# Value and output-gate projections with weight tiles of 512 rows by 512 columns instead of 1024 by 256

## The chip, the core and the metric

The kernel runs on one core of a Trainium2 chip. The metric is the time of one execution on the device in microseconds (us), from its first to its last instruction and what the launch adds around it. TensorE (PE) multiplies; VectorE (DVE) and ScalarE (ACT) work on its results; GpSimd (POOL) and SyncE (SP) mostly issue transfers.

## What is computed

The reference is one layer of a backbone over 256 context rows and 2048 latent rows of 1024 columns. The part that the change touches is the combined input projection:

```python
hl = modulate(rmsnorm(xl, g_norm1[layer]), ml[0], ml[1])
hc = modulate(rmsnorm(xc, g_norm1[layer]), mc[0], mc[1])
pl = split_proj(hl @ w_in[layer])       # 512-column groups: B, C, x_in, q, k, v, o, and 16 gates
pc = split_proj(hc @ w_in[layer])
hm_c, hm_l = mlstm_bidir((pc[3], pc[4], pc[5], pc[7]), (pl[3], pl[4], pl[5], pl[7]), gate_b[layer])
yl = mixer(pl, hm_l, conv_rows, conv_w[layer], conv_b[layer], g_head[layer], w_out[layer])
...
def mlstm_out(h, o, g_head, dtype):
    hn = h * lax.rsqrt(jnp.mean(h * h, axis=-1, keepdims=True) + EPS) * g_head[None, :, None, :]
    ...
    return jax.nn.sigmoid(o) * hn
```

`v` is the value projection (columns 2560 to 3071 of `w_in`), `o` the output gate (columns 3072 to 3583). After the mixer follow the output projection, a router and a mixture of 16 experts with 256 tokens each, and a last RMSNorm.

## The kernel before

Every float32 product is made of three products in the fp32r type: the weight and the activation are each split into a high part (rounded by ACT) and a low part (the remainder, by DVE), and high by high, high by low and low by high are summed in PSUM.

The first part goes over four blocks of 512 latent rows (loop at L548); block 0 also takes the 256 context rows. The normalised rows lie transposed in SBUF as eight tiles of 128 features by 512 rows, `his` and `los`. Weights come as tiles of 1024 rows by 256 columns, 1 MB each: `wtile` (L407) loads one over the SP queue into one of two `wraw` slots, `split_w` (L89) makes `whi` on ACT and `wlo` on DVE in one of three slots each. Two helpers multiply. `wstat` (L411) holds the weights still and moves 512 rows of `h`: 24 products of 512 columns for a result tile. `hstat` (L422) holds 128 rows of `h` still and moves the 256 columns of the weight tile: 24 products of 256 columns for a result tile of 128 rows by 256 columns. `hstat` is used for `v` (L564 to L574) and `o` (L646 to L655), each as two weight tiles (`j`) with four row tiles (`t`) for each, and in block 0 two more row tiles of the context for `v` (L568). A block has 14 weight tiles: K, V, Q, O with two each, then two rounds of three for the convolution. Result tiles lie in the PSUM pool `pmm`, four banks (L149), which the gates (L293) and the modulation rows (`pq`, L633 and L641) use too.

`v` is copied by DVE into `V1s` (L574), from which the scan's state is updated (`state_update`, L435) and which ACT's queue stores to `PK`. `o` goes through a Sigmoid on ACT into `so` (two slots of 256 columns), is multiplied on POOL by the head gain (L653) and stored from ACT's queue to `PG` (L655). Ahead of each `o` tile stands `mod_tile` (L631), which computes 256 columns of a modulation row on DVE from a 1 MB tile of `w_mod`, loaded into the same `wraw` slots.

The order on each engine is not the program's: the context at L1273 has `schedule_with_timeline_sim=True`, so a planner puts the instructions in order by a timeline of its own and gives out the slots. From some 745 us the scan's second half and the output projection (`stage_b`, L703, products of 512 columns at L730 to L732) follow, then the router, then the experts: `psx` at L1192 to L1194 with products of 256 columns, and `down` (L1106) with products of 512 columns over four PSUM tiles in turn, 128 rows of `h` held and split weights moved.

Of the kernel before, what the change touches and what calls it, by code (L numbers as in the profile page):

```python
# [8 lines left out]
F32 = mybir.dt.float32  # L9
# [4 lines left out]
AF = mybir.ActivationFunctionType  # L14
# [5 lines left out]
P = 128  # L20
D = 1024
KD = D // P
SEQ = 2048
NCTX = 256
NH = 4
# [13 lines left out]
def kernel(ctx, tc, x, c, cx, c_ctx, w_mod, b_mod, g_norm1, g_norm2, w_in, w_out, conv_w, conv_b,  # L39
                       gate_b, g_head, w_router, w_gate_e, w_up_e, w_down_e, g_final, out):  # L40
    nc = tc.nc
    V, S, G, T = nc.vector, nc.scalar, nc.gpsimd, nc.tensor
# [3 lines left out]
    w_in = w_in[0]  # L46
# [11 lines left out]
    PG = [dram.tile([P, PKW - SO], F32, name=f"PG{i}") for i in range(NCH)]  # L58
# [25 lines left out]
    def load_w(src, rows, cols):  # L84
        raw = wrawp.tile([P, rows, cols], F32, name="wraw", tag="wraw")
        nc.sync.dma_start(raw, src)
        return raw

    def split_w(raw, rows, cols, after=None, after_lo=None):  # L89
        hi = whip.tile([P, rows, cols], F32R, name="whi", tag="whi")  # L90
        if after is not None:
            S.activation(hi[:, 0, 0:1], after, AF.Copy)
        S.activation(hi, raw, AF.Copy)  # L93
        lo = whip.tile([P, rows, cols], F32R, name="wlo", tag="wlo")
        if after_lo is not None:
            tc.keep_in_program_order(G.tensor_copy(lo[:, 0, 0:1], after_lo))
        V.tensor_sub(lo, raw, hi.bitcast(F32))  # L97
        return hi, lo
# [33 lines left out]
    ghb = con.tile([P, 512], F32, name="ghb")  # L132
# [11 lines left out]
    def pool(st, name, bufs, **kw):  # L144
        return st.enter_context(tc.tile_pool(name=name, bufs=bufs, reuse_waits="tile", **kw))

    hp = pool(left, "hT", 12)
    wl = pool(left, "p1l", 2)
    pmm = pool(left, "p1mm", 4, space=PSUM)  # L149
# [97 lines left out]
    hc, stc = ([], []), [None, None]  # L247
    h, sth = ([], []), [None, None]
# [158 lines left out]
    def wtile(n0):  # L407
        raw = load_w(w_in[:, n0:n0 + 256].rearrange("(k p) n -> p k n", p=P), KD, 256)
        return split_w(raw, KD, 256)

    def wstat(w, i, h, ntok):  # L411
        hi, lo = w
        his, los = h
        ps = pmm.tile([P, 512], F32, name="ps", tag="mm")
        for k in range(KD):
            wh = hi[:, k, i * P:(i + 1) * P]
            T.matmul(ps[:, :ntok], wh, his[k], start=k == 0, stop=False)  # L417
            T.matmul(ps[:, :ntok], wh, los[k], start=False, stop=False)  # L418
            T.matmul(ps[:, :ntok], lo[:, k, i * P:(i + 1) * P], his[k], start=False, stop=k == KD - 1)  # L419
        return ps  # L420

    def hstat(w, h, t):  # L422
        hi, lo = w
        his, los = h
        ps = pmm.tile([P, 512], F32, name="ps", tag="mm")
        for k in range(KD):
            hh = his[k][:, t * P:(t + 1) * P]
            T.matmul(ps[:, :256], hh, hi[:, k, :], start=k == 0, stop=False)  # L428
            T.matmul(ps[:, :256], hh, lo[:, k, :], start=False, stop=False)  # L429
            T.matmul(ps[:, :256], los[k][:, t * P:(t + 1) * P], hi[:, k, :], start=False, stop=k == KD - 1)  # L430
        return ps

    Cst = {}

# [32 lines left out]
    V1c = [V1cc[:, 0], V1cc[:, 1]]  # L467
# [80 lines left out]
    for blk in range(4):  # L548
        KT = wk.tile([P, NH, 512], F32, name="KT", bufs=1)
        for j in range(2):  # L550
            w = wtile(2048 + j * 256)
            if blk == 0:
                for i in range(2):
                    ps = wstat(w, i, hc, NCTX)
                    S.activation(KTc[:, j * 2 + i, :], ps[:, :NCTX], AF.Copy)
            for i in range(2):
                ps = wstat(w, i, h, 512)
# [3 lines left out]
            T.transpose(pv[:, :24], vrow2, ident[:24, :24])  # L561
            V.tensor_copy(vcol[:, 72:96], pv[:, :24])
        V1s = [wk.tile([P, NH, P + 1], F32, name="V1", bufs=4) for _ in range(4)]
        for j in range(2):  # L564
            w = wtile(2560 + j * 256)
            if blk == 0:
                for t in range(2):
                    ps = hstat(w, hc, t)  # L568
                    V.tensor_copy(V1c[t][:, j * 2:j * 2 + 2, 0:P], ps[:, :256].rearrange("p (h v) -> p h v", h=2))
            for t in range(4):  # L570
                if j == 0:
                    V.memset(V1s[t][:, :, P:P + 1], 1.0)
                ps = hstat(w, h, t)
                V.tensor_copy(V1s[t][:, j * 2:j * 2 + 2, 0:P], ps[:, :256].rearrange("p (h v) -> p h v", h=2))  # L574
        if blk == 0:
            gc = gates(hc, 2, None)
        gl = gates(h, 4, blk)
# [4 lines left out]
        for j in range(2):  # L582
            w = wtile(1536 + j * 256)
            for i in range(2):
                ps = wstat(w, i, h, 512)
                qt = wl.tile([P, 512], F32, name="qt", tag="hf", bufs=2)
                S.activation(qt, ps, AF.Copy, scale=P ** -0.5)
                for t in range(4):
                    o_ = QO + (j * 2 + i) * P
# [41 lines left out]
        def mod_tile(q, row=row):  # L631
            def ev_b(acc, dst=(ml2b if row == 2 else ml5b), q=q):
                pq = pmm.tile([P, 512], F32, name="pq", tag="mm")  # L633
                bq = wl.tile([1, 256], F32, name="bq", bufs=2)
                nc.gpsimd.dma_start(bq, b_mod[0:1, row * D + q * 256:row * D + (q + 1) * 256])
                T.matmul(pq[:, :256], ones, acc, start=True, stop=False)
                T.matmul(pq[:, :256], ones[0:1, :], bq, start=False, stop=True)
                S.activation(dst[:, q * 256:(q + 1) * 256], pq[:, :256], AF.Copy)

            def ev_c(acc, dst=(B2 if row == 3 else A2), q=q, v0=(40 if row == 3 else 48)):  # L640
                pq = pmm.tile([P, 512], F32, name="pq", tag="mm")  # L641
                for i in range(2):
                    T.matmul(pq[:, i:i + 1], acc[:, i * P:(i + 1) * P], ones[:, 0:1], start=True, stop=True)
                V.tensor_tensor(dst[:, q * 2:q * 2 + 2], vcol[:, v0 + q * 2:v0 + q * 2 + 2], pq[:, 0:2], op=ALU.add)
            mod_row_bcast(psm, wl, row, q, ev_b if row in (2, 5) else ev_c)
        for j in range(2):  # L646
            mod_tile(j)
            w = wtile(3072 + j * 256)
            for t in range(4):
                so = wl.tile([P, 256], F32, name="so", bufs=2)  # L650
                ps = hstat(w, h, t)
                S.activation(so, ps[:, :256], AF.Sigmoid)
                G.tensor_mul(so, so, ghb[:, j * 256:(j + 1) * 256])  # L653
                o_ = j * 256
                nc.scalar.dma_start(PG[blk * 4 + t][:, o_:o_ + 256], so)  # L655
        for j in range(2):
            mod_tile(2 + j)
            cs = []
            w = wtile(512 + j * 256)
            for i in range(2):  # L660
                ps = wstat(w, i, h, 512)
# [3 lines left out]
            w = wtile(1024 + j * 256)  # L665
            ys = []
            for i in range(2):
                ct = j * 2 + i
                ps = wstat(w, i, h, 512)
# [11 lines left out]
            w = wtile(j * 256)  # L681
            for i in range(2):
                ct = j * 2 + i
                y = ys[i]
                ps = wstat(w, i, h, 512)
# [3 lines left out]
        h = hnext  # L689
# [140 lines left out]
    for n_, k2 in enumerate((2, 3, 0, 1)):  # L830
        raw = load_w(w_out[k2 * 2 * P:(k2 + 1) * 2 * P, :].rearrange("(k p) n -> p k n", p=P), 2, D)
        if n_ < 3:
            hi = whip.tile([P, 2, D], F32R, name="whi", tag="whi")
            lo = whip.tile([P, 2, D], F32R, name="wlo", tag="wlo")
        else:
            hi = wk.tile([P, 2, D], F32R, name="whi3", bufs=1)
            lo = wk.tile([P, 2, D], F32R, name="wlo3", bufs=1)
# [159 lines left out]
    with tc.tile_pool(name="xw", bufs=2, reuse_waits="tile") as xraw, tc.tile_pool(name="xh", bufs=2, reuse_waits="tile") as xhi, \  # L997
# [159 lines left out]
        for e in range(NE):  # L1157
# [4 lines left out]
            for pr in range(npair):  # L1162
                n = 2 if pr < npair - 1 else NFT - 2 * (npair - 1)
                f0 = pr * 2
                ws = []
                for src in (w_gate_e, w_up_e):
                    raw = load_w(src[0, e][:, f0 * P:(f0 + n) * P].rearrange("(k p) n -> p k n", p=P), KD, n * P)
# [18 lines left out]
                for i in range(n):  # L1186
                    ps = pmm.tile([P, 2, 2 * P], F32, name="psx", tag="mm")
                    for m_ in range(2):
                        hi, lo = ws[m_]
# [10 lines left out]
                    hh = wk.tile([P, 2 * P], F32R, name="hh", bufs=4)  # L1200
# [76 lines left out]
```

## Time and profile before

| what | us |
|---|---|
| median of 3 runs | 2697.55 (2696.11 to 2704.61) |
| the profiled execution | 2698.35 |
| span of its instructions | 2696.3 |
| PE busy | 2615.3 (97%) |
| PE weight loads busy, beside the products | 2365.0 (88%) |
| DVE busy | 1584.3 (59%) |
| ACT busy | 1155.3 (43%) |

Products overlap in the records: the busy time of one (280 ns for 256 columns, 390 ns for 512) is from its start to its modelled end, while the next one starts earlier. What a product costs in a full stretch is the distance from its start to the start of the next, and that is read from the timeline.

### The profile page before, as it was taken

The page shows a single profiled execution, that of the slowest core. Times are in us where ns is not written, and L with a number is a line of the kernel's source. Part 1 is how long each engine was busy: PE and PEld are TensorE (multiplying, and loading weights), DVE is VectorE, ACT ScalarE, POOL GpSimd, SP SyncE. Part 2 cuts the span into 40 slices and gives each one's busy share as a digit, 9 for nine tenths or more (in the row PEclk, how much of TensorE's full clock was granted, in tenths as well). Part 3 has the DMA queues.
Part 4 walks back from the last instruction along what each step waited for, and adds up shares of the span by engine and source line. Part 5 has one row for each costly group of instructions (what it writes and reads, how often), then busy time and mean ns, then how long its engine had stood idle before and what let it go on. Part 6 is the DMA issues. An engine that isn't in the chain of part 4 may idle for free.

```text
span 2696.3 us, 42922 instructions
## 1 busy us (share of the span) xinstructions
PE 2615.3 (97%) x17570; PEld 2365.0 (88%) x17570; DVE 1584.3 (59%) x2570; ACT 1155.3 (43%) x1723; POOL 301.0 (11%) x345
## 2 busy tenths in 40 slices
PE   8999999999999999689999999999999999999997
PEld 4988888888878888579999999999999999999987
DVE  5356454554575665566566556656655665665684
ACT  3243333422534444354444444444444444444553
POOL 1010000000111111210011011001101100110231
PEclk9999999999999999889999999999999999999999
DMA  8444554645656655165666666666666666666894
GB/s 271 135 147 148 170 165 147 196 129 156 204 183 206 208 183 172 64 219 188 205 217 208 200 209 219 189 208 214 209 202 208 219 191 206 214 210 202 276 318 166
DMA packets 382532, 524.57 MB, mean 195 GB/s; under 512 B 15072, under 2 KB 322736, under 8 KB 380288
## 3 DMA queue, kind: packets, MB, share of 16 engines
q1 hardware_dynamic: 327968, 437.96, 50.0%
q10 hardware_dynamic: 43792, 46.55, 5.1%
q0 software_dynamic: 10576, 37.32, 5.0%
q8 instruction: 138, 2.26, 0.3%
q14 instruction: 58, 0.48, 0.1%
HBM read 449.05 MB, written 72.61 MB: 193 GB/s over the span
## 4 chain that ended last, share of the span: by engine, by line
PE 63%; DMA 3%; DVE 2%; issue 2%; ACT 0%; POOL 0%; POOLq 0%; DVEq 0%; SPq 0%; ACTq 0%
PE psx L1192 12%; PE psx L1194 11%; PE psx L1193 11%; PE ac L1117 6%; PE ac L1119 6%; PE ac L1118 6%; PE po L730 2%; PE po L732 2%; PE po L731 2%; DMA pk<-PK 1%; PE ptx L1055 1%; PE pl L766 1%; PE pb L514 1%; PE pa L510 1%; DMA ACC<-yv,idx 1%
## 5 line engine op out<-in xcount | busy, mean ns | idle before, releaser
L1192 PE MATMUL psx<-xh,whi 128*128 128x256 f32 x2816 | 788.9, 281 | 1.6 <-ACT whi L93 1.5
L1193 PE MATMUL psx<-xl,whi 128*128 128x256 f32 x2816 | 786.7, 280 | 0.9 <-DVE xl L1064 0.9
L1194 PE MATMUL psx<-xh,wlo 128*128 128x256 f32 x2816 | 787.5, 280 | 0.0
L97 DVE TENSOR_TENSOR wlo<-wraw,whi 128x2048 fp32r<-128x2048 f32 x248 | 532.0, 2156 | 307.8 <-ACT whi L93 304.7
L93 ACT ACTIVATE whi<-wraw 128x2048 fp32r<-128x2048 f32 x248 | 446.7, 1804 | 373.3 <-PE psx L1193 112.1
L1194 PEld LDWEIGHTS psx<-xh,wlo 128*128 128x128 f32 x2816 | 535.3, 190 | 0.1
L1193 PEld LDWEIGHTS psx<-xl,whi 128*128 128x128 f32 x2816 | 530.5, 188 | 3.3 <-DVE xl L1064 1.4
L1192 PEld LDWEIGHTS psx<-xh,whi 128*128 128x128 f32 x2816 | 528.7, 188 | 4.1 <-ACT whi L93 1.7
L1117 PE MATMUL ac<-dhi,hh 128*128 128x512 f32 x704 | 276.2, 392 | 0.0
L1118 PE MATMUL ac<-dlo,hh 128*128 128x512 f32 x704 | 274.7, 390 | 0.0
L1119 PE MATMUL ac<-dhi,hl 128*128 128x512 f32 x704 | 273.3, 390 | 0.0
L1077 DVE TENSOR_TENSOR dlo<-draw,dhi 128x2048 fp32r<-128x2048 f32 x96 | 202.9, 2114 | 114.2 <-ACT dhi L1075 114.2
L418 PE MATMUL ps<-hlo,whi 128*128 128x512 f32 (+1 forms) x672 | 259.6, 387 | 0.0
L419 PE MATMUL ps<-hhi,wlo 128*128 128x512 f32 (+1 forms) x672 | 259.0, 386 | 0.0
L417 PE MATMUL ps<-hhi,whi 128*128 128x512 f32 (+1 forms) x672 | 258.6, 388 | 0.0
L1147 POOL DMA_INDIRECT ACC<-yv,idx x28 | 82.8, 2956 | 1124.1 <-DVE yv L1142 1012.6
L1075 ACT ACTIVATE dhi<-draw 128x2048 fp32r<-128x2048 f32 x96 | 170.2, 1772 | 69.7 <-PE ac L1119 67.6
L1201 ACT ACTIVATE hh<-sgt 128x256 fp32r<-128x256 f32 x176 | 73.2, 417 | 263.0 <-DVE sgt L1197 263.0
L1196 ACT ACTIVATE sgt<-psx 128x256 f32<-128x256 f32 x176 | 65.4, 372 | 228.0 <-PE psx L1194 227.9
L1119 PEld LDWEIGHTS ac<-dhi,hl 128*128 128x128 f32 x704 | 132.1, 188 | 27.8
L428 PE MATMUL ps<-whi,hhi 128*128 128x256 f32 x544 | 156.0, 287 | 0.0
L429 PE MATMUL ps<-wlo,hhi 128*128 128x256 f32 x544 | 154.9, 285 | 0.0
(411 smaller groups left out, 3901.8 us busy)
## 6 DMA issues: line engine op xcount, KB each, us to landing
wraw<-in_w_gate_e_dram SPq DMA_DIRECT2D x80, 1024.0 KB, 6.2
wraw<-in_w_up_e_dram SPq DMA_DIRECT2D x80, 1024.0 KB, 5.5
draw<-in_w_down_e_dram SPq DMA_DIRECT2D x80, 1024.0 KB, 6.1
wraw<-in_w_in_dram SPq DMA_DIRECT2D x56, 1024.0 KB, 5.5
pk<-PK SPq DMA_DIRECT2D x16, 1284.0 KB, 7.7
xt<-in_x_dram SPq DMA_DIRECT2D x32, 512.0 KB, 5.5
wraw<-in_w_mod_dram SPq DMA_DIRECT2D x16, 1024.0 KB, 6.8
wm<-in_w_mod_dram SPq DMA_DIRECT2D x8, 1024.0 KB, 12.0
```

The costliest lines, as they stand in the source:

```text
L93: S.activation(hi, raw, AF.Copy)
L97: V.tensor_sub(lo, raw, hi.bitcast(F32))
L417: T.matmul(ps[:, :ntok], wh, his[k], start=k == 0, stop=False)
L418: T.matmul(ps[:, :ntok], wh, los[k], start=False, stop=False)
L419: T.matmul(ps[:, :ntok], lo[:, k, i * P:(i + 1) * P], his[k], start=False, stop=k == KD - 1)
L1077: V.tensor_sub(lo, raw, hi.bitcast(F32))
L1117: T.matmul(ac, hhs, dh[:, i, sl], start=f == 0, stop=False)
L1118: T.matmul(ac, hhs, dl[:, i, sl], start=False, stop=False)
L1119: T.matmul(ac, hls, dh[:, i, sl], start=False, stop=f == NFT - 1)
L1192: T.matmul(ps[:, m_], wh, xh[:, k], start=k == 0, stop=False)
L1193: T.matmul(ps[:, m_], wh, xl[:, k], start=False, stop=False)
L1194: T.matmul(ps[:, m_], lo[:, k, i * P:(i + 1) * P], xh[:, k], start=False, stop=k == KD - 1)
```

## The change

For `v` and `o` the two weight tiles of 1024 rows by 256 columns become two of 512 rows by 512 columns. `hstat` now makes the result tiles of all row tiles at once: for the first half of the rows it adds to each of them in turn, then for the second half. Each product moves 512 columns and fills a whole PSUM bank. `so` becomes 512 columns wide and shares the two slots of `cs`, the convolution's tile. The first two modulation tiles of a block now both stand ahead of `o`.

```diff
-    def hstat(w, h, t):
-        hi, lo = w
+    def whalves(n0):
+        ws = []
+        for kh in range(2):
+            raw = load_w(w_in[kh * 512:(kh + 1) * 512, n0:n0 + 512].rearrange("(k p) n -> p k n", p=P), 4, 512)
+            ws.append(split_w(raw, 4, 512))
+        return ws
+
+    def hstat(ws, h, ts):
         his, los = h
-        ps = pmm.tile([P, 512], F32, name="ps", tag="mm")
-        for k in range(KD):
-            hh = his[k][:, t * P:(t + 1) * P]
-            T.matmul(ps[:, :256], hh, hi[:, k, :], start=k == 0, stop=False)
-            T.matmul(ps[:, :256], hh, lo[:, k, :], start=False, stop=False)
-            T.matmul(ps[:, :256], los[k][:, t * P:(t + 1) * P], hi[:, k, :], start=False, stop=k == KD - 1)
-        return ps
+        pss = [pmm.tile([P, 512], F32, name="ps", tag="mm") for _ in ts]
+        for kh, (hi, lo) in enumerate(ws):
+            for t, ps in zip(ts, pss):
+                for k4 in range(4):
+                    k = kh * 4 + k4
+                    hh = his[k][:, t * P:(t + 1) * P]
+                    T.matmul(ps, hh, hi[:, k4, :], start=k == 0, stop=False)
+                    T.matmul(ps, hh, lo[:, k4, :], start=False, stop=False)
+                    T.matmul(ps, los[k][:, t * P:(t + 1) * P], hi[:, k4, :], start=False, stop=k == KD - 1)
+        return pss
...
-        for j in range(2):
-            w = wtile(2560 + j * 256)
-            if blk == 0:
-                for t in range(2):
-                    ps = hstat(w, hc, t)
-                    V.tensor_copy(V1c[t][:, j * 2:j * 2 + 2, 0:P], ps[:, :256].rearrange("p (h v) -> p h v", h=2))
-            for t in range(4):
-                if j == 0:
-                    V.memset(V1s[t][:, :, P:P + 1], 1.0)
-                ps = hstat(w, h, t)
-                V.tensor_copy(V1s[t][:, j * 2:j * 2 + 2, 0:P], ps[:, :256].rearrange("p (h v) -> p h v", h=2))
+        ws = whalves(2560)
+        if blk == 0:
+            for t, ps in enumerate(hstat(ws, hc, (0, 1))):
+                V.tensor_copy(V1c[t][:, :, 0:P], ps.rearrange("p (h v) -> p h v", h=NH))
+        for t in range(4):
+            V.memset(V1s[t][:, :, P:P + 1], 1.0)
+        for t, ps in enumerate(hstat(ws, h, range(4))):
+            V.tensor_copy(V1s[t][:, :, 0:P], ps.rearrange("p (h v) -> p h v", h=NH))
...
         for j in range(2):
             mod_tile(j)
-            w = wtile(3072 + j * 256)
-            for t in range(4):
-                so = wl.tile([P, 256], F32, name="so", bufs=2)
-                ps = hstat(w, h, t)
-                S.activation(so, ps[:, :256], AF.Sigmoid)
-                G.tensor_mul(so, so, ghb[:, j * 256:(j + 1) * 256])
-                o_ = j * 256
-                nc.scalar.dma_start(PG[blk * 4 + t][:, o_:o_ + 256], so)
+        for t, ps in enumerate(hstat(whalves(3072), h, range(4))):
+            so = wl.tile([P, 512], F32, name="so", tag="cs", bufs=2)
+            S.activation(so, ps, AF.Sigmoid)
+            G.tensor_mul(so, so, ghb)
+            nc.scalar.dma_start(PG[blk * 4 + t][:, 0:512], so)
```

## Rows read from the trace of the kernel before

**Rows 1.** The page, part 1: busy time of each engine (share of the span) xinstructions.
```profile
PE 2615.3 (97%) x17570; PEld 2365.0 (88%) x17570; DVE 1584.3 (59%) x2570; ACT 1155.3 (43%) x1723; POOL 301.0 (11%) x345
```

**Rows 2.** Busy time by stretch: stretch, its length, engines, PEclk, DMA share, GB/s.
```profile
83.00:745.00 662.00, 659.67 (x3906) 576.17 (x3906) 340.74 (x664) 229.09 (x285) 41.09 (x62) 1.00 0.52 162
```

**Rows 3.** The page, part 5: one of hstat's three product lines (L429, L430 count alike).
```profile
L428 PE MATMUL ps<-whi,hhi 128*128 128x256 f32 x544 | 156.0, 287 | 0.0
```

**Rows 4.** Timeline of PE: hstat's 192 products for `v`, block 1 (start us, us, instruction).
```profile
280.29 0.28 PE L428 MATMUL ps<-whi,hhi 128*128 128x256 f32 x1
...
303.32 0.39 PE L295 MATMUL pg<-hhi,wgp 128*32 128x512 f32 x1
```

**Rows 5.** Timeline of PE: wstat's products for K, just before them.
```profile
269.63 0.39 PE L418 MATMUL ps<-hlo,whi 128*128 128x512 f32 x1
...
280.06 0.39 PE L419 MATMUL ps<-hhi,wlo 128*128 128x512 f32 x1
```

**Rows 6.** Timeline of PE: the 24 products of one `down`.
```profile
1320.79 0.39 PE L1117 MATMUL ac<-dhi,hh 128*128 128x512 f32 x1
...
1326.00 0.40 PE L1119 MATMUL ac<-dhi,hl 128*128 128x512 f32 x1
```

**Rows 7.** Timeline of PE: products of the output projection.
```profile
1103.24 0.39 PE L732 MATMUL po<-whi,yl 128*128 128x512 f32 x1
...
1108.05 0.39 PE L732 MATMUL po<-whi,yl 128*128 128x512 f32 x1
```

**Rows 8.** Timeline of PE: 60 products of 256 columns in the experts' stage.
```profile
1327.61 0.28 PE L1194 MATMUL psx<-xh,wlo 128*128 128x256 f32 x1
...
1334.41 0.28 PE L1194 MATMUL psx<-xh,wlo 128*128 128x256 f32 x1
```

**Rows 9.** Groups by line: what empties the result tiles now, and nearest rows of 512 columns.
```profile
L653 POOL TENSOR_TENSOR so<-so,ghb 128x256 f32<-128x256 f32 x32 | 26.2, 820 | 222.5 <-ACT so L652 194.5 <-issue 22.4 <-DMA PG<-so 5.6
...
L574 DVE COPY V<-ps 128x256 f32<-128x256 f32 x32 | 13.5, 422 | 31.8 <-PE ps L430 31.8
...
L652 ACT ACTIVATE so<-ps 128x256 f32<-128x256 f32 x32 | 12.3, 385 | 33.9 <-PE ps L430 13.4 <-DVE V L572 8.6 <-DVE Cst L453 6.3
...
L587 ACT ACTIVATE qt<-ps 128x512 f32<-128x512 f32 x16 | 9.4, 587 | 40.2 <-PE ps L419 40.2
```

**Rows 10.** The page, part 6, transfers: count, KB each, median us from issue to landing.
```profile
PK<-V ACTq DMA_DIRECT2D x16, 258.0 KB, 6.1
PK<-KT ACTq DMA_DIRECT2D x16, 256.0 KB, 3.6
```

**Rows 11.** Timeline of ACT: weight splits (block 0's second V tile; block 1's two O tiles).
```profile
69.73 1.91 ACT L93 ACTIVATE whi<-wraw 128x2048 fp32r<-128x2048 f32 x1
...
304.20 1.92 ACT L93 ACTIVATE whi<-wraw 128x2048 fp32r<-128x2048 f32 x1 [10.29 <-DMA wraw<-in_w_in_dram]
319.48 1.92 ACT L93 ACTIVATE whi<-wraw 128x2048 fp32r<-128x2048 f32 x1 [0.24 <-PE ps L418]
```

**Rows 12.** Timeline of SP: block 1's second load of modulation weights.
```profile
298.80 0.37 SPq L86 DMA_DIRECT2D wraw<-in_w_mod_dram  x1
```

**Rows 13.** Timeline of PE: first product of `v` (block 0), of `pq`, of `o` (block 1).
```profile
83.28 0.28 PE L428 MATMUL ps<-whi,hhi 128*128 128x256 f32 x1
...
332.44 0.50 PE L643 MATMUL pq<-ones,macc 128*128 128x1 f32 x4
332.81 0.37 PE L428 MATMUL ps<-whi,hhi 128*128 128x256 f32 x1
```

**Rows 14.** Timeline of PE: two of four idle times over 0.25 us in the blocks.
```profile
362.58 0.60 PE L447 MATMUL pU<-V,wkk 128*128 128x129 f32 x3 [0.48 <-DVE V L572]
...
488.44 0.72 PE L301 MATMUL p<-sel,gsb 32*128 32x16 f32 x5 [1.03 <-DVE gsb L298]
```

**Rows 15.** PE's longest idle time at the end of the blocks.
```profile
792.61 1.23 PE L514 MATMUL pb<-pk,mb 128*128 128x129 f32 x4 [3.83 <-DVE mb L500]
```

**Rows 16.** Busy time by stretch, columns as in Rows 2: the stretch behind it.
```profile
792.00:800.00 8.00, 7.13 (x36) 6.94 (x36) 6.85 (x10) 3.73 (x8) 0.00 (x0) 0.60 0.68 220
```

## The prediction

> **What bounds the kernel now.** I read the page's busy times first [rows 1]: PE is at work in 97% of the span, DVE in 59%, ACT in 43%. The stretch that the change touches is read next, by windows [rows 2]: in the 662 us of the four blocks PE stands idle for 662.00 - 659.67 = 2.33 us, at a granted clock of 1.00, and DVE and ACT have half of the time and more to spare. So in this stretch the time is the sum of the distances from one product to the next, and only what shortens those distances or removes an idle time counts. The timeline of PE has these distances; the mean duration in a group row, 287 ns for a product of 256 columns [rows 3], does not, because products overlap in the records.
>
> **The products.** Each of `hstat`'s three lines runs 544 times [rows 3]: 4 blocks x 4 weight tiles x 4 row tiles x 8, and 2 x 2 x 8 for the context. That is 1632 products of 256 columns. In block 1 the 192 products for `v` stand in one row without anything between them, and take 303.32 - 280.29 = 23.03 us [rows 4]: 119.9 ns each. All of them: 1632 x 0.1199 = 195.7 us.
>
> After the change the same sums need half as many products of 512 columns: 816. Three places have the price of one. `wstat` in the same stage, with the roles of weights and rows exchanged: 46 steps in 280.06 - 269.63 = 10.43 us [rows 5], 226.7 ns. `down` in the experts' stage, with the roles as the change has them (128 rows of `h` held, split weights moved, the PSUM bank changed after every three products): 23 steps in 5.21 us [rows 6], 226.5 ns. The output projection, also with the roles as the change has them: 21 steps in 4.81 us [rows 7], 229.0 ns. I take 226.7, since the first row is from the same stage, beside the same loads and splits, and the second has the same form of work. 816 x 0.2267 = 185.0 us. **The saving is 195.7 - 185.0 = 10.7 us**; at the output projection's price it is 195.7 - 186.9 = 8.8 us. All of it lies on PE's path.
>
> **Rule and row.** A pair of products now costs 2 x 119.9 = 239.8 ns and the one that takes its place 226.7: 13.1 ns are saved for each pair, and so about that much of a product's cost does not go with its columns. [...]
>
> **The weight tiles.** Number (14 for each block), size (1 MB), loads, splits on ACT (1.92 us each) and on DVE stay as they are; only the rectangle changes. A tile's products now take 48 x 0.2267 = 10.9 us for four row tiles where they took 96 x 0.1199 = 11.5 us, so slots come free in the same rhythm. What hides the splits is a lead of two tiles: the high parts of block 1's two O tiles are made at 304.20 and 319.48 [rows 11], and the first product with them starts at 332.81 [rows 13], 13 us after the second of them began. Block 0 is the tight place. There the context's row tiles need the second tile after 24 x 0.2267 = 5.4 us, where it was needed after 17.3 us (144 x 0.1199), and the first tile stays in its slot until the latents have used it. But the second tile's split starts at 69.73 [rows 11], and `v` starts only once K is done, at 83.28 [rows 13]. Cost 0; without this cover it would be one split's wait, 2 us.
>
> **The results.** 36 copies of `v` on DVE at 0.42 us become 18 of 512 columns, 32 Sigmoids at 0.385 us become 16 at some 0.59 us (the nearest row, L587), and 32 products on POOL at 0.82 us become 16 at some 1.6 us by their columns [rows 9]. Each engine has less work in total, but nothing of it is on PE's path: DVE waits 31.8 us for PE before these copies. Cost and gain 0.
>
> **The banks.** This is the new wait. `pmm` has four banks, and a stretch for four row tiles now holds all four from its first half to its second. The first bank is full 5/8 of the way, 8.2 us before the stretch ends, and emptying takes some 0.6 us [rows 9], so the next user finds it free. At the start, the fourth bank is needed three row tiles (8.2 us) after the first. What is queued behind: the modulation products (`pq`), which need a bank of the same pool and cannot run in a stretch's first half. Two of them stand ahead of `o` instead of one. The second's weights are loaded at 298.80 [rows 12], 34 us ahead of `o`, and the first's product runs at 332.44, just before `o` [rows 13]; I price the second there at 0, as its sum on DVE is long done by then, and at up to 4 us for each block if a planner puts it late.
>
> **The gate's store.** `so` now waits for one of two slots until the tile before last has landed: Sigmoid 0.6, POOL 1.6, landing 3.6 to 6.1 us for stores of that size [rows 10], together 5.8 to 8.3 us, while two row tiles take PE 12 x 0.2267 x 2 = 5.4 us. ACT stands up to 3 us for each of the last two, and with it the queue behind: the convolution's copies, the next split, the stores. Who waits for that is PE, but with the two tiles of lead above and four banks, that is over 10 us of cover. Cost 0; without the cover 3 to 6 us for each block.
>
> **The order.** The planner lays the work out anew, so the idle times may go elsewhere. In the blocks there are four over 0.25 us, 2.3 us in all, with 1.03 us as the longest [rows 14]: that is all that can be gained there. [...]
>
> **The sum.** 2698.35 - 10.7 = 2687.65 us against the profiled execution. That execution is 0.8 us over the median of the runs shown, so beside the median it is 2686.9. I write 2687.5.
>
> **The rivals.** A measurement of this kernel can tell some 0.3%, 8.1 us, from no change; so "faster" is below 2689.5 and "slower" above 2705.6.
>
> *The saving is made, but part of it is given back.* If one stop like that at 792.61 is added, or each block pays 2 us for a late `pq` or for ACT's wait, 7 to 8 us come back: 2687.5 + 8 = 2695.5. For it: the saving has only 2.6 us to spare over the bound, and the gates' chain already stops PE twice behind DVE's queue [rows 14]. Against it: every cover above is 5 us or more.
>
> *The price goes by columns.* The trace has products of 256 columns at two levels: 119.9 ns in `hstat`, but 60 of them in (1334.41 - 1327.61) = 6.80 us in the experts' stage [rows 8], 113.3 ns, which is exactly half of 226.7. If whatever lifts 113.3 to 119.9 here lies in this stage's use of the memories and not in the number of products, it may lift 512 columns to 239.8 too, and the time stays: 2697.5. Against it: `wstat` reads the same tiles in the same stage at 226.7 [rows 5].
>
> *Slower: the banks stop PE.* All four banks are held, and the bank that comes next is emptied by an engine that stands in a queue (ACT behind a store's landing, DVE behind splits and sums). PE then stops between stretches, and the clock falls behind each stop: 7.0 us, as at 792.61 [rows 15, 16]. There are eight stretches. Two stops give back more than the saving (14.0 against 10.7); from three on the kernel is slower: 2687.5 + 21.0 = 2708.5; one in each block gives 2687.5 + 28.0 = 2715.5. Against it: `down` also goes over four banks in turn, at 226.5 ns without an idle time [rows 6]. [...]
>
> **How the numbers follow.** The sum as it stands has 0.60: most of its range, 2683 to 2689.5, is "faster". Part given back has 0.22 and the price by columns 0.07: both "same", 2689.5 to 2698. The stops have 0.11, at 2706 to 2716. So faster 0.60, same 0.29, slower 0.11. Low end: the saving, the 2.3 us of idle time and a part of the 7.0 us stop, 2687.5 - 5 = 2682.5. High end: the saving at 8.8 us and one and a half added stops, 2689.4 + 10.5 = 2700. That leaves out the stops (0.11) and little else.
>
> **What would show it.** Right: 816 products of 512 columns on the new line, at 226 to 230 ns from start to start, 96 of them for `v` in 21.8 us in blocks 1 to 3, and the end of the blocks some 10 us earlier. The second step: PE's idle time in the blocks still some 2 us. Wrong: 240 ns from start to start; idle times before the new line, the gates' products or `pq` with ACT or DVE as the releaser; ACT idle before `so` until a `PG` store lands; a granted clock below 1.00 in the blocks, or a longer stop where 3.83 us stood.

## The result, and the profile after

The changed kernel takes 2684.72 us (median), the kernel before, run again beside it, 2699.47 us. The medians differ by 14.8 us; the ratio is 0.9941, with an interval of 0.9929 to 0.9954, which is 16 us faster, between 12 and 19. One of the six executions of the changed kernel took 3839 us, at a mean granted clock of 0.63, and is left out of the ratio. The profiled executions say 2684.5 against 2698.35 us, with spans of 2682.8 and 2696.3 us: 13.5 us less. The forecast was 2687.5 us, the range 2682.5 to 2700, so the time lies inside it.

First the busy times (page, part 1) and the four blocks by windows, as in [rows 1, 2].

```profile
PE 2603.4 (97%) x16754; PEld 2319.8 (86%) x16754; DVE 1587.2 (59%) x2552; ACT 1139.0 (42%) x1694; POOL 299.7 (11%) x329
```
```profile
82.83:735.00 652.17, 651.37 (x3094) 533.35 (x3094) 343.96 (x644) 207.92 (x243) 36.41 (x42) 1.00 0.50 162
```

There are 816 products fewer, PE is as busy as before, and in the blocks it stands idle for 652.17 - 651.37 = 0.80 us where it was 2.33 us [rows 2]. The granted clock is 1.00 in this execution.

Now the timeline of PE at the `v` products of block 1, which answers to [rows 4]: 96 products between these two rows.

```profile
278.27 0.39 PE L437 MATMUL ps<-whi,hhi 128*128 128x512 f32 x1
...
300.03 0.39 PE L295 MATMUL pg<-hhi,wgp 128*32 128x512 f32 x1
```

21.76 us, 226.7 ns from one to the next, where 192 products took 23.03 us.

What empties the results, as group rows of the same stretch (answering to [rows 9]), and the store of `so` from the page of transfers (answering to [rows 10]):

```profile
L657 POOL TENSOR_TENSOR so<-so,ghb 128x512 f32<-128x512 f32 x16 | 22.7, 1420 | 211.6 <-ACT so L656 203.7 <-issue 7.8
...
L580 DVE COPY V<-ps 128x512 f32<-128x512 f32 x16 | 10.9, 686 | 5.0 <-PE ps L439 5.0
L656 ACT ACTIVATE so<-ps 128x512 f32<-128x512 f32 x16 | 9.6, 597 | 19.9 <-PE ps L439 8.8 <-POOL so L657 4.8 <-DMA PG<-so 4.4
```
```profile
PG<-so ACTq DMA_DIRECT2D x16, 256.0 KB, 2.0
```

ACT stands 4.8 + 4.4 = 9.2 us in all before `so`, until POOL or the store lets it go on. Only a part of this is new: in the kernel before ACT stood 5.1 us in two waits for the same store (view of L652), and what is added are two waits for POOL. PE does not show either. Its one idle time over 0.25 us in the blocks is another one, and the longest behind the blocks (answering to [rows 15]) is nearly as it was:

```profile
187.92 0.80 PE L456 MATMUL pU<-V1c,wkk 128*128 128x129 f32 x5 [0.80 <-DVE wkk L447]
...
780.05 0.75 PE L523 MATMUL pb<-pk,mb 128*128 128x129 f32 x4 [3.60 <-DVE mb L509]
```

Where the 13.5 us of span went, read from the timelines of both: the last `wstat` product starts at 787.04 before and 774.72 after, 12.3 us earlier. The output projection ends 12.0 us earlier. At the start of the experts' stage the kernel before has an idle time that the changed one hasn't:

```profile
1182.98 0.39 PE L1192 MATMUL psx<-xh,whi 128*128 128x256 f32 x1 [1.55 <-ACT whi L93]
```

The lead is 11.8 us when this stage begins, 13.9 us behind its first expert, and 13.5 at the end.

### The profile page after: what moved, and what is told of

Read it like the earlier page. It is cut to its first block, busy times and chain, and to the rows that moved or that the text cites. A ratio compares the mean times of both kernels' runs of the same rounds, so it can differ in the third digit from the quotient of the medians.

```text
span 2682.8 us, 41178 instructions
## 1 busy us (share of the span) xinstructions
PE 2603.4 (97%) x16754; PEld 2319.8 (86%) x16754; DVE 1587.2 (59%) x2552; ACT 1139.0 (42%) x1694; POOL 299.7 (11%) x329
## 4 chain that ended last, share of the span: by engine, by line
PE 84%; DMA 4%; DVE 2%; issue 2%; ACT 1%; POOL 0%; POOLq 0%; SPq 0%; DVEq 0%; ACTq 0%
PE psx L1195 12%; PE psx L1197 11%; PE psx L1196 11%; PE ac L1122 6%; PE ac L1120 6%; PE ac L1121 6%; PE ps L417 4%; PE ps L419 4%; PE ps L418 4%; PE po L733 2%; PE po L735 2%; PE po L734 2%; PE ps L439 2%; PE ps L437 2%; PE ps L438 2%
## 5 line engine op out<-in xcount | busy, mean ns | idle before, releaser
L1121 PEld LDWEIGHTS ac<-dlo,hh 128*128 128x128 f32 x704 | 132.3, 188 | 23.6
L1120 PEld LDWEIGHTS ac<-dhi,hh 128*128 128x128 f32 x704 | 132.2, 188 | 23.6
```

Of the source, the lines that this page charges most:

```text
L1120: T.matmul(ac, hhs, dh[:, i, sl], start=f == 0, stop=False)
L1121: T.matmul(ac, hhs, dl[:, i, sl], start=False, stop=False)
```

## An account of the blocks

The experiments are read by one account, worked out from PE's timeline for each kernel, between the first product of `v` in block 0 and the last product of `wstat` in block 3. The length of that stretch is the sum of the distances from product to product. For each form of product (a line of the kernel with one shape) I take its median distance times its number; what is left over is the excess: idle times, what a fall of the granted clock costs, and what a change from one kind of product to another costs. The excess hangs on the grouping: by shape alone it is 10.7 us for the kernel before, 6.8 after, 7.5 for e1 and 7.8 for e10. So it is good to some 3 us, and smaller differences are read from the stretch itself. Times are us.

| kernel | its `hstat` products | stretch | those products | excess | PE idle |
|---|---|---|---|---|---|
| before | 1632 of 256 | 703.8 | 195.8 | 9.5 | 2.3 |
| after | 816 of 512 | 691.6 | 185.2 | 6.9 | 0.8 |
| e4_again | 816 of 512 | 693.3 | 185.2 | 8.7 | 1.0 |
| e1_two_256 | 1632 of 256 | 700.1 | 195.8 | 4.8 | 0.0 |
| e10_before_mods_ahead | 1632 of 256 | 700.3 | 195.8 | 5.0 | 0.0 |
| e2_v_only | 768 of 256, 432 of 512 | 701.9 | 190.1 | 13.4 | 4.1 |
| e3_o_only | 864 of 256, 384 of 512 | 698.1 | 190.9 | 7.7 | 1.5 |
| e6_bank_turns | 816 of 512 | 692.2 | 185.2 | 7.8 | 1.0 |
| e9_mods_apart | 816 of 512 | 691.3 | 185.2 | 6.8 | 0.0 |
| e7_two_banks | 816 of 512 | 690.6 | 185.2 | 6.0 | 0.0 |

The fourth column goes by width and number alone and is the same wherever these are. The fifth moves between 4.8 and 13.4; e2 stands out in either grouping. Ratios below are against the kernel before, run beside each kernel.

## Experiments

**e1_two_256.** The products alone are undone; tiles, banks and the order of the halves stay.

```diff
-                    T.matmul(ps, hh, hi[:, k4, :], start=k == 0, stop=False)
+                    for c0 in range(0, 512, 256):
+                        cs_ = slice(c0, c0 + 256)
+                        T.matmul(ps[:, cs_], hh, hi[:, k4, cs_], start=k == 0 and c0 == 0, stop=False)
...
```

> The changed kernel with its weight tiles of 512 by 512, its four banks and its order of halves, but each product of 512 columns made as two of 256. Theory (each product costs some 13 ns beside its columns): 1632 products at 119.9 ns again, 10.7 us more than the changed kernel, some 2695 us, with the new products 120 ns from start to start and idle times in the blocks as in the changed kernel (0.8 us). Rival (the gain comes from the new order and tiles, the width does little): it stays within 3 us of the changed kernel, 2684 to 2688 us. Rival (a 256-column product's price hangs on how its weight tile lies in memory): 113 ns from start to start, 226 for a pair, and no loss against the changed kernel.

Measured: 2698.0 us, ratio 0.9979 (0.9970 to 0.9988), 12.0 us over the changed kernel run beside it (2686.0). The same stretch of PE's timeline, 192 products between the two rows:

```profile
279.82 0.28 PE L440 MATMUL ps<-whi,hhi 128*128 128x256 f32 x1
...
302.85 0.39 PE L295 MATMUL pg<-hhi,wgp 128*32 128x512 f32 x1
```

23.03 us, 119.9 ns each, as before to the last digit. The other rectangle of the tile does nothing for a product of 256 columns, and the width is what gives the gain. The third theory (113 ns by the place in memory) falls. The 12.0 us are near the theory's 10.7 in part by luck. The stretch is only 6.8 us longer than that of e4_again and 8.5 longer than that of the first profile: this order has no idle time in the blocks, which I had not expected. But PE stops at the start of the experts' stage, with the granted clock at 0.94 over the 30 us around it (1161.5 to 1191.5 us), and that stage is 5.2 us longer than in e4_again:

```profile
1179.85 0.58 PE L1198 MATMUL psx<-xh,whi 128*128 128x256 f32 x1 [2.65 <-ACT whi L93]
```

So what shows the width's share are the products (10.6 us), not the difference of the two times.

**e2_v_only and e3_o_only.** Each half of the change alone, the other one as in the kernel before.

```diff
e2_v_only:
-        for t, ps in enumerate(hstat(whalves(3072), h, range(4))):
+        for j in range(2):
+            mod_tile(j)
+            w = wtile(3072 + j * 256)
...
e3_o_only:
-        ws = whalves(2560)
+        for j in range(2):
+            w = wtile(2560 + j * 256)
...
```

> The change for the value projection alone; the output gate as in the kernel before. Theory: 864 of 1632 products are halved, 432 x 13.1 ns = 5.7 us less than the kernel before, ratio 0.998, and about 5 us more than the changed kernel; the idle times can move it by 2 us. Rival (order): no share in proportion, anything between no gain and the whole 13.5 us of span.

> The change for the output gate alone; the value projection as in the kernel before. Theory: 768 of 1632 products are halved, 384 x 13.1 ns = 5.0 us less than the kernel before, ratio 0.998; with the other half alone it should sum up to the 10.7 us of both. Rival (order): the part of the gain over 10.7 us (about 3 us of idle time that is gone) comes with one of the two halves, which then gains 8 us or more.

Measured: `v` alone 2700.74 us, ratio 0.9991 (0.9982 to 1.0000), some 2 us less than before; `o` alone 2695.24 us, ratio 0.9970 (0.9958 to 0.9982), some 8 us less. In the products both did as computed: 190.1 and 190.9 us, so 5.7 and 4.9 less than 195.8. But the times aren't in that proportion, as the rival (order) said; its mark of 8 us for one half is just reached by `o`. By the ratios the two halves alone sum to 10.5 us where both together gave 17.8 beside them. The account says why for `v`: its excess is 13.4 us. These are PE's waits over 0.25 us in its blocks (waits, PE alone: waiting line, releaser, us in total, times, longest):

```profile
PE p L301 <- DVE gsb L298: 1.5, 1, 1.5
PE pU L467 <- DVE V L589: 1.4, 2, 0.8
PE pt L176 <- DVE hf L185: 0.9, 1, 0.9
```

All three are the small chains of the gates, the state and the next rows, behind DVE's queue. The first two are at places that the kernel before has too [rows 14], where they take 1.3 and 1.0 us in all; the third is new. Behind the first one the granted clock fell too: 0.89 over 655 to 670 us, which is 15 x 0.11 = 1.7 us more. The stretch is 1.9 us shorter than the kernel before's where the products alone make it 5.7, so 3.8 us went back; more idle time (4.1 us against 2.3) and this fall of the clock are 3.5 of them. The new order cost here more than half of what the width had saved.

**e4_again.** The changed kernel beside the others.

> The changed kernel once more, beside the others on the same chip: ratio 0.9945 with some 0.001 to either side by all theories; it is what the other three are read against.

Measured: 2686.0 us, ratio 0.9934 (0.9921 to 0.9948). Its profiled stretch is 1.7 us longer than the first time, with the same instructions, and the trace shows where: in block 0 the granted clock fell as `o` began, behind two modulation results and other small products, without an idle time of PE (windows, columns as in [rows 2]).

```profile
150.00:160.00 10.00, 10.00 (x42) 7.80 (x42) 5.50 (x13) 1.48 (x4) 1.05 (x2) 0.83 0.69 210
```

10 x 0.17 = 1.7 us. Products of 512 columns lie 426 ns apart there (7 steps from 152.49 to 155.47 us). The first profile has the same order and 1.00 in the same 10 us, so this comes in some executions and not in others.

**e10_before_mods_ahead.** The kernel before, with the one part of the change that is order alone.

```diff
         for j in range(2):
             mod_tile(j)
+        for j in range(2):
             w = wtile(3072 + j * 256)
```

> The kernel before with one part of the change alone: both first modulation tiles of a block ahead of the output gate; its weight tiles, its 1632 products of 256 columns and its banks stay. Theory: no share of the 10.6 us; within 4 us of the kernel before either way, ratio 0.9985 to 1.0015. Rival (the order is the gain): 3 us or more faster than the kernel before.

Measured: 2698.3 us, ratio 0.9985 (0.9976 to 0.9994), 4 us less than before: at the edge between theory and rival. The products are 195.8 us, the excess 5.0, without any idle time in the blocks. The stretch is 3.4 us shorter than the kernel before's, with the same products. So an order without PE's 2.3 us of idle time was to be had without any new width.

**e9_mods_apart.** The changed kernel, the second modulation tile behind the output gate again.

```diff
-        for j in range(2):
-            mod_tile(j)
+        mod_tile(0)
         for t, ps in enumerate(hstat(whalves(3072), h, range(4))):
...
+        mod_tile(1)
```

> The changed kernel with the second modulation tile of each block put behind the output gate again, so that one pq stands ahead of the four banks and not two; products and tiles are unchanged. Theory: the sum of the distances is the same (185.2 us for the 816 products), and the time moves only by what the planner's new order does at the joints, within 4 us of the changed kernel. Rival (moving the modulation ahead is what gave the gain beyond 10.6 us): 3 us or more are lost, with idle times before the output gate or behind it.

Measured: 2684.29 us, ratio 0.9938 (0.9924 to 0.9951), within a microsecond or two of the changed kernel; excess 6.8 to its 6.9, no idle time. With the new products the place of this tile is worth nothing that shows. The rival falls for this kernel, though moving the tile went with a gain in the old one (e10). So the tile's place does not carry this part by itself; that the planner's order as a whole does is what is left, and not shown further.

**e6_bank_turns.** The bank changes after every three products, and all four results end within the last 2.1 us of a stretch.

```diff
-            for t, ps in zip(ts, pss):
-                for k4 in range(4):
+            for k4 in range(4):
+                for t, ps in zip(ts, pss):
```

> The changed kernel with the PSUM bank changed after every three products (the four row tiles in the inner loop, the four features tiles in the outer) instead of after every twelve; all four results then end within 2.1 us of the end of the stretch. Theory: 227 ns from start to start at a granted clock of 1.00, as in the experts' down products; the banks are emptied in the time that the gates' products or the next weights' first result take, so at most 1 us for each of 8 stretches, 0 to 8 us in all, and any loss stands as idle time at the ends of the stretches. Rival (turning through the banks makes PE pause and its clock fall): the granted clock in the blocks falls below 1.00 and the loss is 7 us for each stop, over 20 us in all.

Measured: 2686.02 us, ratio 0.9945 (0.9932 to 0.9959), as the changed kernel. The blocks by windows, and PE's waits in them:

```profile
83.00:770.00 687.00, 686.05 (x3268) 562.29 (x3267) 368.38 (x678) 224.49 (x287) 43.48 (x48) 1.00 0.51 164
```
```profile
PE pg L295 <- DVE V L580: 1.0, 3, 0.5
```

The granted clock is 1.00, the distance 226.7 ns. The bank's handover now does stop PE, where expected: the gates' products wait for the copy of `v` in blocks 1 to 3, 0.5 us at most and 1.0 in all, without a fall of the clock.

**e7_two_banks.** Two banks held instead of four.

```diff
-        for t, ps in enumerate(hstat(whalves(3072), h, range(4))):
+        ws = whalves(3072)
+        for t, ps in ((t0 + i, p_) for t0 in (0, 2) for i, p_ in enumerate(hstat(ws, h, (t0, t0 + 1)))):
...
```

> The changed kernel with the four row tiles of a block taken two at a time, so that two banks are held and not four, and both weight tiles stay in their slots until the second pair is done. Theory: the distances stay 227 ns, and since four held banks cost nothing that shows, two give nothing back: within 4 us of the changed kernel, the excess over the sum of the distances in the blocks between 5 and 9 us. Rival (the four held banks cost): 3 us or more faster, excess below 4 us.

Measured: 2683.07 us, ratio 0.9927 (0.9910 to 0.9944). The lowest median of all, but its interval and that of the changed kernel in e4_again (0.9921 to 0.9948) overlap nearly whole. Excess 6.0, no idle time. Holding four banks costs nothing that can be told here; the rival's 3 us lie at the edge of what these medians can tell, and its excess below 4 us did not come.

**e5_four_128.** The cost of a product by itself, at a third width.

```diff
+                    for c0 in range(0, 512, 128):
+                        cs_ = slice(c0, c0 + 128)
...
```

> The changed kernel with each product of 512 columns made as four of 128: 3264 products. It measures the cost by itself. [...]

Measured: one execution, 2902.05 us, and the law of 13 ns beside the columns fell. The timeline of PE in `v` of block 0:

```profile
89.45 0.28 PE L440 MATMUL ps<-whi,hhi 128*128 128x128 f32 x1
...
91.79 0.28 PE L440 MATMUL ps<-whi,hhi 128*128 128x128 f32 x1
```

21 steps in 2.34 us: 111.4 ns, where a straight line through 119.9 ns at 256 columns and 226.7 at 512 gives 66.5 at 128. In all 3264 such products cost 365.6 us by their median, 180.3 more than 816 of 512. The stretch is 208 us longer than the changed kernel's. The 28 us beyond the products go with a fall of the granted clock: it is 0.96 over the blocks and 0.50 from 184 to 224 us, though PE was never idle there. There the same products lie some 213 ns apart (11 steps from 185.61 to 187.96 us), as far as products of 256 columns do at a granted clock of 0.50 in the experts' stage (after, 9 steps from 2553.25 to 2555.17 us).

**e11_384_128.** A fourth width, to tell two laws apart above that floor: at 384 columns the straight line through 119.9 ns at 256 and 226.7 at 512 gives 173.3 ns, three quarters of the 226.7 are 170.0; the 0.172 of the sum below lies between them.

```diff
+                    for c0, c1 in ((0, 384), (384, 512)):
+                        cs_ = slice(c0, c1)
...
```

> The changed kernel with each product of 512 columns made as one of 384 and one of 128, in groups of three of either kind. It gives a fourth width. Products of 128 columns lay 111 ns apart in e5_four_128, so the law of 13 ns beside the columns fell there, and a floor of 111 ns shows. [...] In all 816 x (0.172 + 0.111) = 231 us, 46 us more than the changed kernel, if the two widths cost the same mixed as alone.

Measured: one execution, 2734.22 us. The timeline of PE in the same place:

```profile
90.03 0.40 PE L440 MATMUL ps<-whi,hhi 128*128 128x384 f32 x1
90.26 0.34 PE L441 MATMUL ps<-wlo,hhi 128*128 128x384 f32 x1
90.44 0.34 PE L442 MATMUL ps<-whi,hlo 128*128 128x384 f32 x1
90.61 0.22 PE L440 MATMUL ps<-whi,hhi 128*128 128x128 f32 x1
90.67 0.27 PE L441 MATMUL ps<-wlo,hhi 128*128 128x128 f32 x1
90.78 0.28 PE L442 MATMUL ps<-whi,hlo 128*128 128x128 f32 x1
90.89 0.39 PE L440 MATMUL ps<-whi,hhi 128*128 128x384 f32 x1
```

The distance from the second 384 to the third has a median of 175 ns over the run, nearer to the straight line (173.3) than to three quarters of 226.7 (170.0). The change of width blurs it: the first start after 128 columns lies early, so that 232 and 60 ns stand where 175 and 111 would. Six products take some 0.86 us together, 234 us for all 816 pairs, against 231 expected. I take the straight line above the floor as likely, not as shown.

## Why the prediction was right, and where it was not

*The products* held to the nanosecond: in the unbroken stretches of `v` they lie 226.7 ns apart, and all 816 by their median make 185.2 us against 185.0, a saving of 10.6 us against 10.7. The two rows that I chose to price them, `wstat` in the same stage and `down` with the same roles [rows 5, 6], were the right ones; the output projection's 229.0 [rows 7] was not reached. e1 undoes this step alone: its products are back at 119.9 ns, and it loses 12.0 us, of which some 5 lie in the experts' stage and so are not the width's. The rival that a product of 512 columns would rise to 239.8 is refuted by the profile after. But why 256 columns cost 113.3 ns in the experts' stage [rows 8] stays open; at that price this change would have saved nothing.

*What the 13 ns are* I had too simply, as a part of a product's cost that goes with neither columns nor anything else. e5 refutes that at 128 columns, which lie 111.4 ns apart. At a granted clock of 0.50 128 and 256 columns cost the same, some 213 ns (e5, after), so a floor is likely there; and 512 columns cost 425 ns (before, 2 steps from 2568.56 to 2569.41 us), less than twice 226.7, so the 13 ns are not a fixed number of clocks either. The forecast did not rest on this, since both its widths were priced from rows of their own. What sets the floor is not shown: in e5 each product brings its own 128 columns of weights, whose load takes 192 ns in the records (median, L441) and overlaps the products, and no run here left the loads out.

*The weight tiles* cost nothing, as priced. *The banks* cost nothing either: the first two modulation results run just before `o`, as forecast, and e6 makes the handover visible at 1.0 us in all. The slower rival had its price from a stop with a fall of the clock [rows 15, 16]; the handover stops PE for half a microsecond at most, and the clock stays. That turning through the banks makes the clock fall was not shown: with a change of bank every three products the granted clock in the blocks is 1.00. What the prediction did not price is the fall of the clock at the start of `o` that e4_again shows behind the two modulation results: 1.7 us, in one of two profiled executions.

*The gate's store*: the wait is there, as forecast, and hidden, as forecast, but it was not all new: the kernel before had 5.1 us of it. Two of its terms were bounded too high: POOL takes 1.42 us and not 1.6, and the landing has a median of 2.0 us and not 3.6 to 6.1, for stores of the same size [rows 10]; why those take longer is not shown. ACT stood 9.2 us in all where up to 3 us for each of eight tiles would have been 24. The bound for one tile was too low: the longest wait is the 4.4 us for the store.

*The order* is the term that was mis-sized. I priced it at 0 in the sum and said that at most 2.3 us could be gained in the blocks. There it brought 1.5 us (idle time 2.33 to 0.80). But I had looked for such joints in the blocks and at their end only; 1.5 us more came at the start of the experts' stage, where the wait for the split of the first weights is gone. 10.6 + 1.5 + 1.5 = 13.6 is near the 13.5 us of span; that it comes so near is in part luck, since the lead also moves by some tenths either way between these stages. The runs show how loose this term is: with the same number of products of each width the stretch went from 700.1 to 703.8 us (e1, e10 and before). The rival in which part is given back was not what the change did, but e2 shows that it was a real one: there between 3 and 4 of 5.7 us went back, to DVE's queue before the gates' chain, the place that the prediction had named, and to the fall of the clock behind it. That stop cost 1.5 + 1.7 = 3.2 us, less than half of the 7.0 that the prediction put on one. Those 7.0 us are 3.83 of idle time and 8 x 0.40 = 3.2 by the clock [rows 15, 16]; no run shows an added stop at that price, and after the change the stop in the same place comes to 3.60 + 8 x 0.21 = 5.3 us, at a granted clock of 0.79 over 780 to 788 us. And the room that this rival was given, 2.6 us up to the bound, is counted from 2686.9; from the 2687.5 of the forecast it is 2.0.

Open is the rest between the spans (13.5 us) and the ratio (12 to 19 us): the other executions of the kernel before lie up to 8.5 us above its fastest, the profiled one is near the low end, and no trace of a higher one was taken. Open too is why the planner's order comes out better or worse for a given edit; e9 and e10 show only that the modulation tile's place is not the reason by itself.

## What to carry to other kernels

Where PE is never idle, price an edit by the distance from one product's start to the next, taken from a row with the same form and the same roles; here it held to a per cent. Moving 512 columns for each load of weights instead of 256 saved 13 ns of 240 here, and the banks that it holds cost nothing, as they were emptied by the time of their next use (after: PE's one wait over 0.25 us in the blocks is for `wkk`). In the experts' stage of the same kernel a stretch of products of 256 columns lies at 113.3 ns [rows 8], where this would save nothing, so the price of the narrow product is to be read in its own stage. Where a planner orders the work, any edit moves the joints as well: undo the edit with the rest left in place (as e1), and count the products in the trace besides, since the undone kernel has joints of its own. Here 10.6 of the 13.5 us of span belonged to the width.

## What the runs showed of the hardware

Distances of fp32r products that each bring their own 128 by 128 weights, in the projections and at full clock: 111.4 ns for 128 columns (e5), 119.9 for 256 (before, e1), about 175 for 384 (e11), 226.7 for 512 (after). At a granted clock of 0.50: some 213 ns for 128 (e5, 184 to 224 us) and for 256 (after, experts' stage, 2553.25 to 2555.17 us), 425 for 512 (before, experts' stage, 2568.56 to 2569.41 us). Going from 512 columns down to 256 costs 6% for the same work, down to 128 nearly a factor of two (446 ns for 227). Turning through four PSUM banks every three products (e6) left both the distance (226.7 ns) and the granted clock (1.00) as they were. And the clock fell without an idle time of PE: to 0.50 over 184 to 224 us in a stream of products of 128 columns (e5), and behind a few small products in one execution and not in another with the same instructions (0.83 over 150 to 160 us in e4_again, 1.00 in after).
